# Moving the sample group's memory attention from the attention stage into the projection's second half

## The chip, the cores and the metric

The kernel runs on one core of one Trainium2 chip. The metric is the device time of one execution in microseconds (us): the median of several runs. One more execution is taken with the hardware profiler; all rows of "the profile" and "the trace" come from it.

## The reference

One layer of a hybrid decoder for a prompt of 2048 tokens and a sample group of 8 sequences of 4 new tokens each (8 x 4 = 32 rows). A combined projection `z = RMSNorm(x) @ w_in` gives eleven column groups of 512: `ca, cb, cg` (convolution), `pu, pg` (pooling), `q, k, v, sg` (stick-breaking attention), `mq, mg` (memory attention). Each branch is gated by its own SiLU path; the four branches are concatenated, multiplied by `w_out`, normalised and added to the residual.

The branch that the change touches is the memory attention of the sample group: each of the 8 sequences has its own 256 memory tokens, with keys `cache_mem_k` and values `cache_mem_v` of 4 heads x 128:

```python
def mem_attend(q, mk, mv):
    s = jnp.einsum('nqhd,nmhd->nhqm', q, mk).astype(jnp.float32) * (MEM_HEAD_DIM ** -0.5)
    p = jax.nn.softmax(s, axis=-1)
    return jnp.einsum('nhqm,nmhd->nqhd', p.astype(mv.dtype), mv)
...
y_m = mem_attend(mq.reshape(n, l, MEM_HEADS, MEM_HEAD_DIM), mk, mv).reshape(n, l, W_MEM)
mix = jnp.concatenate([..., y_m * jax.nn.silu(mg)], axis=-1)
```

## The kernel before

Three stages follow one another.

**Projection.** The normalised, transposed input lies in SBUF (`xhi`, `xlo`), 1024 prompt tokens plus the 32 sample rows in the first half (part 0), the other 1024 prompt tokens in the second (part 1). `z_groups` goes through column groups of 128: for each it runs `mm3` (24 matmuls on PE) per tile of up to 512 tokens into one of two PSUM banks (`z_tile`, pool `zps`), and `z_evac` empties the bank with ACT and DVE. It yields twice per tile; such a yield is called a step here. At each step `tasks.step()` lets every live task emit its next piece (turning rows, the prompt's memory attention `mem_attend`, pooling, the depthwise convolution `conv_dw` on DVE), and a planner (`due`, `rate`) lets the sample group's paged attention (`sample_stages`: gathers on POOL's queue, 32 x 32 turns on DVE, scores `sSA` and values `sO` on PE in strips) advance so that it ends shortly before the projection. Tasks take PSUM banks from a pool of three (`tp_tile`, pool `tps`), and SBUF tiles by tag: four of 4 KB per partition (`k4`), four of 2 KB (`small`).

The order of the instructions on PE is the order in which the code emits them. On the other engines the framework orders them by its own cost model and inserts all waits; each engine, and SP's DMA queue, then runs its list in order.

**Attention of the prompt.** `sb_prompt` walks over 4 head pairs x 4 query blocks of 512 tokens x key chunks. Per step: scores `S` on PE, gates `gam` and `be` on ACT, scans `E` on DVE, products on POOL, turns `AT` on PE, copies `at`, values `av` on PE, and at the end of a block one DVE instruction `sbo` (L1385). After the first eight steps `side_work` advances by one yield for every 4.0 cost units: first `sample_mem`, then `sample_end`, then the first output weights; then it waits until head pair 3 begins. Side work takes its PSUM banks from the two `AT` banks of `sb_prompt`. The `S` tiles (two banks each, two of them) lie in the PSUM space that `zps` and `tps` had.

**Output.** The products with `w_out`, the norm and the residual.

The sample group's memory attention is spread over these stages. In the first half the task `sample_keys` loads each sequence's keys (`mkb`, 512 KB) into a `k4` tile, turns them on PE (8 transposes, `smt`), copies them on ACT (`mkbT`) and stores them to DRAM (`mkTd`). It pauses while the prompt's memory attention is at work (`state["att"]`). `sample_mem`, in the attention stage, loads all turned keys, forms the scores of four sequences at a time in one bank (`smS`: per sequence four matmuls, one for each head, in 32-column strips; `qm` holds the queries with zeros at the other sequences' rows so that four sequences add up), adds the two banks into `smsc`, does the softmax, turns the probabilities (`smpt`), multiplies with the values of four sequences at a time (`smO`, all four heads against all 512 columns), masks the right head (`hm`), adds the heads (`smR`), turns the result (`smr`) and gates it into `mixs[3]`.

Of the kernel before, what the change touches and what calls it, by code (L numbers as in the profile page):

```python
# [18 lines left out]
P = 128  # L19
# [68 lines left out]
def kernel(  # L88
# [51 lines left out]
    mkTd = dram.tile([NB, P, 4, NMEM], F32, name="mkTd")  # L140
# [7 lines left out]
    zc = zx.enter_context(tc.tile_pool(name="zc", bufs=1, side="left"))  # L148
    zps = zx.enter_context(tc.tile_pool(name="zps", bufs=2, space=PSUM, side="left"))
    tps = zx.enter_context(tc.tile_pool(name="tps", bufs=3, space=PSUM, side="left"))  # L150
# [34 lines left out]
    us_s = zc.tile([P, 4, NB, CH + TS], F32, name="us_s")  # L185
    ps_s = zc.tile([P, 4, NB, PH + TS], F32, name="ps_s")
# [253 lines left out]
    def sample_keys():  # L440

        for b in range(NB):
            while state["att"]:
                yield
            k_ = k4(f"mkb{b}", [P, 2, 512], F32)
            sp.dma_start(k_, cmk[b].rearrange("(t p) c -> p t c", p=P))
            for _ in range(4):
                yield
            kT = k4(f"mkbT{b}", [P, 4, NMEM], F32)
            for t in range(2):  # L450
                pt = tp_tile(f"smt{b}_{t}")
                for h in range(4):
                    pe.transpose(pt[:, P * h : P * (h + 1)], k_[:, t, P * h : P * (h + 1)], ident)
                act.copy(kT[:, :, P * t : P * (t + 1)], pt.rearrange("p (h n) -> p h n", h=4))
                yield
            wq.dma_start(mkTd[b], kT)

# [159 lines left out]
    def conv_dw(c, U, part):  # L617
# [20 lines left out]
        if part == 0:  # L638
# [14 lines left out]
            wq.dma_start(ydw[c, :, SEQ : SEQ + NS], acc)  # L653

# [10 lines left out]
    state = {"att": 0}  # L665
# [168 lines left out]
    def state_rows(part):  # L834
        yield
        if part == 0:
            tcs = small("tcs")
            tps_ = small("tps")
            for t_, s_, o_ in ((tcs, us_s, CH), (tps_, ps_s, PH)):
                for c in range(4):  # L840
# [7 lines left out]
                      [(TS * b, TS * b + TS, pool_sample[0, b, PH - TS : PH, :]) for b in range(NB)])  # L848
        else:
# [297 lines left out]
    def sample_mem(sm, ps_, S):  # L1147

        qm = sm.tile([P, NB, 4, NS], F32, name="qm", bufs=1)
        pool.memset(qm, 0.0)  # L1150
        for b in range(NB):
            pool.tensor_copy(qm[:, b, :, TS * b : TS * (b + 1)], mqs[:, :, TS * b : TS * (b + 1)])

        h4 = sm.tile([P, 4, 4], F32, name="h4", bufs=1)
        pool.memset(h4, 1.0)
# [5 lines left out]
        for g in (2, 3):  # L1161
            pool.tensor_tensor(out=hm, in0=hm, in1=h4[:, g], op=ALU.add)
# [13 lines left out]
        for k in range(2):  # L1176
# [10 lines left out]
            for b in range(4 * k, 4 * k + 4):  # L1187
                vb[b] = load(b)
# [959 lines left out]
```

## Time and profile before

| | us |
|---|---|
| median of 3 runs | 2398.44 (2398.2 to 2399.28) |
| the profiled execution | 2395.7 |
| its span, first to last instruction | 2394.0 |
| first matmul of the second half's first tile (`z1k`) | 782.7 |
| last first-product matmul of the group `z1sg`, at the end of the projection | 1476.3 |
| last `sbo` of the attention | 1960.6 |

PE is TensorE's matmuls, PEld its weight loads, DVE VectorE, ACT ScalarE, POOL GpSimd, SP SyncE, which here only issues DMAs. `L1385` is line 1385 of the kernel. A form such as `128*32 128x256` of a matmul is its weights (rows * columns) and its moving operand. In the profile an fp32 matmul of two fp32 operands shows as two records; matmuls are pipelined, so a record lasts longer than the distance to the next one.

### The profile page before, as it was taken

What the parts mean: (1) busy time and instruction counts of PE and PEld (TensorE: products, weight loads), DVE (VectorE), ACT (ScalarE), POOL (GpSimd) and SP (SyncE); (2) the same over time, 40 slices, a digit from 0 to 9 for tenths busy, and PEclk for the clock granted to TensorE, in tenths of its full rate; (3) what the DMA queues carried; (4) which work ended last, traced back from release to release, by engine and by line L of the source; (5) the groups of instructions that cost most, each with busy time, mean ns of one, the idle gap of its engine ahead of it and who ended that gap; (6) DMA issues with size and microseconds to landing.
All of it is one profiled execution on the core that took longest, in us unless ns stands there. A gap on an engine that the chain in (4) does not pass through costs nothing. (4 is left out here: it accounts for less than half of the span.)

```text
span 2394.0 us, 42116 instructions
## 1 busy us (share of the span) xinstructions
PE 2275.1 (95%) x15962; PEld 1769.7 (74%) x15962; DVE 1732.6 (72%) x2420; ACT 1117.0 (47%) x1939; POOL 1286.6 (54%) x1323
## 2 busy tenths in 40 slices
PE   7899999999999999999999999899999998989996
PEld 7888888898888777777777776455555557778775
DVE  5332785959756764587877878879898846687998
ACT  5322343242442322224242435788989955443554
POOL 3454535556464655546556554667776754454430
PEclk9999999999999999999999999999999999999998
DMA  6678988887778899978878767834333217887764
GB/s 211 196 253 290 347 287 309 305 269 267 259 256 306 301 357 318 318 270 276 272 268 274 260 222 190 238 77 119 82 93 80 63 63 250 268 284 239 255 236 164
DMA packets 340437, 562.14 MB, mean 235 GB/s; under 512 B 28481, under 2 KB 212929, under 8 KB 323834
## 3 DMA queue, kind: packets, MB, share of 16 engines
q1 hardware_dynamic: 284858, 290.72, 39.2%
q0 software_dynamic: 55376, 268.72, 31.6%
q8 instruction: 126, 2.06, 0.3%
q14 instruction: 77, 0.63, 0.1%
HBM read 469.28 MB, written 90.68 MB: 234 GB/s over the span
## 5 line engine op out<-in xcount | busy, mean ns | idle before, releaser
L974 DVE STREAM_TRANSPOSE T<-kt 128x1024 f32<-128x1024 f32 x256 | 308.5, 1225 | 184.1 <-PE sSA L987 179.4
L941 POOL DMA_INDIRECT vt<-in_cache_v_dram,idv x256 | 252.8, 988 | 255.1 <-PE sO L1026 194.3
L629 DVE SCALAR_TENSOR_TENSOR cacc<-U,par,cacc 128x512 f32<-128x512 f32 x480 | 360.2, 750 | 11.5
L1353 POOL TENSOR_TENSOR be<-be,E 128x512 f32<-128x512 f32 (+3 forms) x316 | 301.2, 960 | 106.1 <-DVE E L1344 45.9
L1344 DVE TENSOR_TENSOR_SCAN E<-gam,cr,ZM 128x513 f32<-128x513 f32 x192 | 233.0, 1264 | 14.8 <-ACT gam L1275 13.5
L941 POOL DMA_INDIRECT kt<-in_cache_k_dram,idk x128 | 128.1, 1001 | 194.3 <-DVE T L974 155.0
L1364 PEld LDWEIGHTS AT<-ident,be 128*128 128x128 f32 x1082 | 115.7, 141 | 128.1 <-ACT at L1370 45.1
L1968 PE MATMUL acc<-wohi,mh 128*128 128x512 f32 (+1 forms) x480 | 194.6, 405 | 2.1 <-DVE mh L1725 1.1
L1275 ACT ACTIVATE gam<-S,nbias_bc 128x1024 f32<-128x1024 f32 (+1 forms) x158 | 171.6, 1086 | 46.0 <-ACT be L1276 17.1
L1968 PE MATMUL acc<-wolo,mh 128*128 128x512 f32 (+1 forms) x480 | 190.8, 397 | 0.0
L1968 PE MATMUL acc<-wohi,ml 128*128 128x512 f32 x448 | 179.0, 400 | 9.8 <-DVE ml L1725 9.6
L1271 PE MATMUL S<-kT,Q 128*128 128x512 f32 (+1 forms) x632 | 175.2, 401 | 4.6 <-DVE sg1sg L727 2.4
L1276 ACT ACTIVATE be<-S,bias_bc 128x1024 f32<-128x1024 f32 (+1 forms) x158 | 170.7, 1080 | 0.0
L1364 PE MATMUL AT<-ident,be 128*128 128x128 f32 x1082 | 156.3, 282 | 15.0 <-DVE at L1368 3.9
L1380 PE MATMUL av<-at,V 128*64 128x512 f32 (+3 forms) x640 | 152.6, 555 | 1.7 <-DVE sbo L1385 1.7
L987 PE MATMUL sSA<-T,W 128*32 128x128 f32 x4096 | 138.4, 276 | 3.2 <-DVE T L974 2.4
L987 PEld LDWEIGHTS sSA<-T,W 128*32 128x32 f32 x4096 | 104.1, 110 | 40.0 <-issue 31.1
L1725 DVE TENSOR_TENSOR ml<-mr,mh 128x512 fp32r<-128x512 f32 x108 | 98.6, 918 | 35.0 <-ACT mh L1714 34.6
L1026 PE MATMUL sO<-vt,saT 128*32 128x512 f32 x1024 | 122.3, 593 | 0.0
L1271 PEld LDWEIGHTS S<-kT,Q 128*128 128x128 f32 x632 | 105.6, 194 | 19.7 <-ACT be L1276 3.4
L1370 ACT COPY at<-AT 128x512 f32<-128x512 f32 x192 | 109.5, 661 | 14.4 <-PE AT L1364 14.4
L1341 DVE TENSOR_TENSOR_SCAN E<-gam,ZM 128x384 f32<-128x384 f32 (+1 forms) x124 | 94.5, 812 | 24.8 <-ACT gam L1275 22.1
(581 smaller groups left out, 6044.3 us busy)
## 6 DMA issues: line engine op xcount, KB each, us to landing
Q<-qd SPq DMA_DIRECT2D x64, 256.0 KB
mr<-mixd SPq DMA_DIRECT2D x32, 512.0 KB
mr<-mixd SPq DMA_DIRECT2D x48, 256.0 KB
wor<-in_w_out_dram SPq DMA_DIRECT2D x20, 512.0 KB
xtp<-in_x_prompt_dram SPq DMA_DIRECT2D x16, 512.0 KB
kT<-kd SPq DMA_DIRECT2D x64, 128.0 KB
wor<-in_w_out_dram SPq DMA_DIRECT2D x32, 256.0 KB
msd<-mr SPq DMA_DIRECT2D x32, 256.0 KB
```

The source lines that it names most:

```text
L629: dve.scalar_tensor_tensor(out=ps, in0=U[:, a + k : a + k + H], scalar=wd[:, k : k + 1], in1=ps, op0=ALU.mult, op1=ALU.add)
L941: pool.indirect_dma_start(out=dst, out_offset=None, in_=rows, in_offset=bass.IndirectOffsetOnAxis(ap=idx, axis=0))
L974: S["turn"] = dve.transpose(T[:, 2 * hh : 2 * hh + 2].rearrange("p s j t -> p (s j t)"), kt[:, 2 * hh : 2 * hh + 2].rearrange("p s j d -> ...
L987: pe.matmul(sSs[n][32 * g : 32 * g + 32, P * ml : P * (ml + 1)], lhsT=W[:, jj, :], rhs=T[:, :, jj, :], start=i == 0, stop=i == 3, tile_pos ...
L1271: pe.matmul(S[:, j, :w], lhsT=Q[:, x, P * (q2 + j) : P * (q2 + j + 1)], rhs=kt[:, :w], start=x == 0, stop=x == 1)
L1275: act.activation(out=ga, in_=S[:, :, :w], func=AF.Sigmoid, bias=nbias_bc[:, h : h + 1], scale=-1.0)
L1276: act.activation(out=be, in_=S[:, :, :w], func=AF.Sigmoid, bias=bias_bc[:, h : h + 1])
L1344: dve.tensor_tensor_scan(out=E[:, j][:, ::-1], data0=g_[:, j][:, ::-1], data1=ZM[:, 0:1].to_broadcast([P, 513]), initial=carry[hh, q2][:, ...
L1353: pool.tensor_tensor(out=be[:, j, :m], in0=be[:, j, :m], in1=E[:, j, 513 - w : 513 - w + m], op=ALU.mult)
L1364: pe.transpose(ap_[:, P * qt : P * (qt + 1)], A[hp, qb, kc, hh, qt][:, P * r : P * (r + 1)], ident)
L1380: pe.matmul(av[64 * hh : 64 * hh + 64, c], lhsT=V[:, 4 * kc + r, 64 * hh : 64 * hh + 64], rhs=ats.pop((hp, qb, kc, r, hh))[:, c], start=dg ...
L1968: pe.matmul(o[:rows], lhsT=m[a][:, k, :rows], rhs=W[prod, 4 * h + k][w], start=not cont and h == k == n == 0, stop=h == 1 and k == 3 and n ...
```

## The change

`sample_keys` and the scratch `mkTd` go. `sample_mem` becomes a task of the projection, added after the key and value groups of the second half, and does everything there. Per sequence: the rows (keys, later values) are loaded one sequence ahead of their use; the keys are turned and copied as before, the scores of this one sequence go into a `tp_tile` bank, and DVE adds them up. After the softmax each sequence's values are multiplied in four strips of 256 columns: two token halves times two pairs of heads, at four partition groups of one bank. ACT copies the bank, and two matmuls against a selector (`Sel`, 128 x 8 ones and zeros) turn it, add the two token halves and pick the right head in one go; DVE gates the result.

For its long-lived tiles it takes the space of the sample's convolution and pooling histories (`us_s`, `ps_s`), so it waits until these are read (`state["early"]` counts four convolutions and two state rows). And the PSUM pool of the turned tiles (`tps`) is opened before that of the projection's output (`zps`), so the two change places among the banks.

```diff
-    mkTd = dram.tile([NB, P, 4, NMEM], F32, name="mkTd")
...
+    tps = zx.enter_context(tc.tile_pool(name="tps", bufs=3, space=PSUM, side="left"))
     zps = zx.enter_context(tc.tile_pool(name="zps", bufs=2, space=PSUM, side="left"))
-    tps = zx.enter_context(tc.tile_pool(name="tps", bufs=3, space=PSUM, side="left"))
...
-    def sample_keys():
...
-    def sample_mem(sm, ps_, S):
...
+    def sample_mem():
+
+        while state["early"] < 6:
+            yield
+        qm = zc.tile([P, NB, 4, NS], F32, tag="us", name="qm", bufs=1)
+        pool.memset(qm, 0.0)
         for b in range(NB):
             pool.tensor_copy(qm[:, b, :, TS * b : TS * (b + 1)], mqs[:, :, TS * b : TS * (b + 1)])
...
+        def rows(src, b, nm):
+            while state["att"]:
+                yield
+            t = k4(f"{nm}{b}", [P, 2, 512], F32)
+            sp.dma_start(t, src[b].rearrange("(t p) c -> p t c", p=P))
             return t

+        ahead = yield from rows(cmk, 0, "mkb")
+        for _ in range(4):
+            yield
         for b in range(NB):
+            k_ = ahead
+            ahead = yield from (rows(cmk, b + 1, "mkb") if b + 1 < NB else rows(cmv, 0, "mvb"))
+            kT = k4(f"mkbT{b}", [P, 4, NMEM], F32)
+            for t in range(2):
+                pt = tp_tile(f"smt{b}_{t}")
                 for h in range(4):
+                    pe.transpose(pt[:, P * h : P * (h + 1)], k_[:, t, P * h : P * (h + 1)], ident)
+                act.copy(kT[:, :, P * t : P * (t + 1)], pt.rearrange("p (h n) -> p h n", h=4))
+                yield
+            yield
+            S = tp_tile(f"smS{b}")
+            for h in range(4):
+                pe.matmul(S[32 * h : 32 * h + 32, :NMEM], lhsT=qm[:, b, h, :], rhs=kT[:, h, :], start=True, stop=True,
+                          tile_position=(0, 32 * h))
+            if b:
                 dve.tensor_tensor(out=sc, in0=sc, in1=S[:, :NMEM], op=ALU.add)
             else:
                 dve.tensor_copy(sc, S[:, :NMEM])
...
+        for b in range(NB):
+            k, g = divmod(b, 4)
+            v_ = ahead
+            if b + 1 < NB:
+                ahead = yield from rows(cmv, b + 1, "mvb")
+            O = tp_tile(f"smO{b}")
             for t in range(2):
+                for c in range(2):
+                    r = 64 * t + 32 * c
+                    pe.matmul(O[r : r + 32, :256], lhsT=pv[:, t, g], rhs=v_[:, t, 256 * c : 256 * c + 256], start=True,
+                              stop=True, tile_position=(0, r))
+            Os = small(f"smOs{b}")
+            act.copy(Os[:, :256], O[:, :256])
+            yield
+            yield
+            yield
+            pt = tp_tile(f"smr{b}")
+            for n in range(2):
+                pe.matmul(pt[:, 2 * TS * n : 2 * TS * (n + 1)], lhsT=Os[:, P * n : P * (n + 1)],
+                          rhs=Sel[:, k, n].rearrange("p c q -> p (c q)"), start=True, stop=True)
+            heads = lambda x: x[:, :, TS * b : TS * (b + 1)].rearrange("p (c n) q -> p n c q", c=2)
+            dve.tensor_tensor(out=heads(mo), in0=pt[:, : 4 * TS].rearrange("p (n c q) -> p n c q", n=2, c=2),
+                              in1=heads(gms), op=ALU.mult)
         sp.dma_start(mixs[3], mo)
...
-        yield from z_groups(0, GROUPS[0][12:14])
-        tasks.add(sample_keys())
-        yield from z_groups(0, GROUPS[0][14:])
+        yield from z_groups(0, GROUPS[0][12:])
         tasks.add(state_rows(0))
-        yield from z_groups(1, GROUPS[1][:-2])
+        yield from z_groups(1, GROUPS[1][:7])
+        tasks.add(sample_mem())
+        yield from z_groups(1, GROUPS[1][7:-2])
...
-        for i, part in enumerate((sample_mem, sample_end)):
-            with tc.tile_pool(name=f"sm{i}", bufs=1, side="left", reuse_waits="tile") as sm2:
-                yield from part(sm2, side_ps, S)
+        with tc.tile_pool(name="sm", bufs=1, side="left", reuse_waits="tile") as sm2:
+            yield from sample_end(sm2, side_ps, S)
```

108 lines of the change are left out of this document (26 added, 82 removed).

## Prediction

> **What bounds the kernel now.** I read the page first, then the busy times by stretch of the span, then PE's timeline at the two places that the change touches: the projection's second half, where it puts the work, and the first 150 us of the attention, where it takes the work away. The page:
>
> ```profile
> span 2394.0 us, 42116 instructions
> PE 2275.1 (95%) x15962; PEld 1769.7 (74%) x15962; DVE 1732.6 (72%) x2420; ACT 1117.0 (47%) x1939; POOL 1286.6 (54%) x1323
> ```
>
> PE is busy 95% of the span, but that is a mean over stages. By stretch (columns: length, then busy us of PE, PEld, DVE, ACT and POOL with their instruction counts, then granted clock, DMA share, GB/s):
>
> ```profile
> 320.00:380.00 60.00, 55.21 (x491) 48.80 (x492) 47.57 (x73) 35.26 (x66) 28.15 (x29) 1.00 0.75 262
> 1000.00:1200.00 200.00, 199.81 (x1512) 148.36 (x1505) 159.14 (x207) 56.16 (x99) 108.09 (x98) 1.00 0.80 272
> ```
>
> The second row is the projection's second half: PE has no idle time (199.81 of 200), while DVE, ACT, POOL and the DMA engines all have some. Whatever PE work is added here moves the end one for one. The first row is where the key transposes of the sample's memory run now, beside a memory head of the prompt: there PE loses 4.79 of 60 us.
>
> The next view is the timeline of PE at the start of the attention, where the scores of the sample's memory (smS) run now. Columns: start, length, engine, line, operation, and in brackets PE's idle time before and what ended it.
>
> ```profile
> 1494.94 0.66 PE L1364 MATMUL AT<-ident,be 128*128 128x128 f32 x4
> 1497.21 0.64 PE L1181 MATMUL smS<-mkbT,qm 128*32 128x256 f32 x8 [1.61 <-DVE at L1368]
> ...
> 1501.74 2.08 PE L1271 MATMUL S<-kT,Q 128*128 128x512 f32 x4
> ...
> 1506.27 1.93 PE L1181 MATMUL smS<-mkbT,qm 128*32 128x256 f32 x32
> 1508.13 0.65 PE L1380 MATMUL av<-at,V 128*64 128x256 f32 x4
> 1508.72 0.66 PE L1364 MATMUL AT<-ident,be 128*128 128x128 f32 x4
> 1511.00 0.63 PE L1364 MATMUL AT<-ident,be 128*128 128x128 f32 x4 [1.62 <-DVE smsc L1184]
> ```
>
> PE's own work ends at 1495.60, then it waits for a bank, works and waits on smS until 1501.74 (6.14 us), gives 1.86 us more from 1506.27, and waits 1.62 us for DVE to empty the bank: 9.62 us of PE for the scores. But PE is not alone there. DVE in the same stretch:
>
> ```profile
> 1484.12 1.00 DVE L1341 TENSOR_TENSOR_SCAN E<-early,ZM 128x128 f32<-128x128 f32 x2 [4.21 <-ACT ZM L1301]
> ...
> 1501.87 0.42 DVE L1186 COPY smsc<-smS 128x256 f32<-128x256 f32 x1 [0.91 <-PE smS L1181]
> 1505.34 0.49 DVE L1368 TENSOR_TENSOR at<-AT,tri 128x128 f32<-128x128 f32 x2 [3.04 <-PE AT L1364]
> 1510.46 0.40 DVE L1184 TENSOR_TENSOR smsc<-smsc,smS 128x256 f32<-128x256 f32 x1
> 1510.89 0.42 DVE L1190 TENSOR_REDUCE smx<-smsc 128x1 f32<-128x256 f32 x1
> ```
>
> From 1484.12 DVE works through its scans almost without a gap; its idle time that smS causes is 0.91 + 3.04 us, and the instructions that go away here are 0.42 + 0.40 + 0.42. So the start-up could be held by DVE rather than PE.
>
> **The change, part by part.**
>
> *Attention, scores.* Out go 9.62 us of PE, but DVE would then be late next: it can move up only by 0.91 + 3.04 + 0.42 + 0.40 + 0.42 = 5.2 us. Bounds 5.2 and 9.6; I take 5.2, because DVE has no other gap there. The sample's last attention part (sample_end) moves up into this place. It has the same instructions as now and takes the same kind of bank; I cost the move at nothing, at worst the 1.61 us bank wait of the smS row.
>
> *Attention, values.* For these I use a yardstick: the instruction that finishes a block of 512 queries of a head pair (sbo, DVE). First head pair, then the third, which has no side work:
>
> ```profile
> 1535.38 0.67 DVE L1385 TENSOR_TENSOR sbo<-av,sgt 128x512 f32<-128x512 f32 x1
> 1574.79 0.66 DVE L1385 TENSOR_TENSOR sbo<-av,sgt 128x512 f32<-128x512 f32 x1
> ...
> 1768.07 0.67 DVE L1385 TENSOR_TENSOR sbo<-av,sgt 128x512 f32<-128x512 f32 x1
> 1800.81 0.67 DVE L1385 TENSOR_TENSOR sbo<-av,sgt 128x512 f32<-128x512 f32 x1
> ```
>
> The same block takes 39.41 us beside the values of the sample's memory and 32.74 us without: 6.7 us go. What is late next is PE itself, as in the clean block.
>
> *PSUM banks.* The attention's first score tile takes the first two banks on the left. Before, these are the two of the projection's output; after, two of the turned tiles, which are free earlier.
>
> ```profile
> 1479.96 3.13 PE L1271 MATMUL S<-kT,Q 128*128 128x512 f32 x8 [2.39 <-DVE sg1sg L727]
> 1481.48 1.12 ACT L1275 ACTIVATE gam<-S,nbias_bc 128x1024 f32<-128x1024 f32 x1 [1.14 <-PE S L1271]
> ```
>
> PE's wait of 2.39 us for the gate sg1sg goes. What is late next is ACT, which waited only 1.14 us for these scores; and DVE's first scan waits for ZM, which ACT makes after these gates. So 1.1 us, at most 2.4, at least 0.
>
> Together the attention gives 5.2 + 6.7 + 1.1 = 13.0 us, at most 9.6 + 6.7 + 2.4 = 18.7. That the later side parts (sample_end, the first output weights) end sooner is worth nothing: in the code they then wait for head pair 3.
>
> *Projection, the strips.* Added to PE's full stream are eight score groups and eight value groups, each 8 matmul records of 256 columns in four strips side by side. What such a group costs inside the stream shows where the paged attention (sSA, 32 records of 128 columns in four strips) interrupts it now; below it, a 128-row, 128-column weight load with a short moving operand, like the new matmuls by the selector:
>
> ```profile
> 1417.64 0.39 PE L243 MATMUL z1mq<-xlo,whi1mq 128*128 128x512 f32 x1
> 1417.87 0.40 PE L243 MATMUL z1mq<-xhi,wlo1mq 128*128 128x512 f32 x1
> 1418.20 1.08 PE L987 MATMUL sSA<-T,W 128*32 128x128 f32 x32
> 1419.21 0.50 PE L243 MATMUL z1mq<-xhi,whi1mq 128*128 128x512 f32 x1
> 1419.55 0.40 PE L243 MATMUL z1mq<-xlo,whi1mq 128*128 128x512 f32 x1
> ...
> L904 PE MATMUL qps<-qsT,rep x32: 192/276/277, 140.0 to 143.4; 128*128 128x32 f32 x32
> ```
>
> The stream's step is 0.23 us (1417.64 to 1417.87). From 1417.87 to 1419.55 are 1.68 us, of which two steps are the stream's own 0.46: the interruption costs 1.22. Its columns alone are half of the long smS run (1.86 us for as many records of twice the columns): 0.93. So 0.29 us are the price of going to strips and back. A group of 8 records is a quarter of the long run, 0.47 us, plus 0.29 when it stands alone: 0.76. Sixteen make 7.5 us (no price of switching) to 12.2 us; I take 12.2, because before, each switch was paid for 16 or 32 records and now for 8.
>
> The Trainium skill, "TensorEngine Tiling (Array Packing)", Key Properties, says that changing the tiling mode drains TensorE; it gives no figure, and by it the sum is that of the upper end, with which the sSA row agrees.
>
> *Projection, the selector.* Each batch adds two matmuls of 8 columns against a 128-column weight, 4 records in fp32; 32 in all. The qps row has 32 records in 3.4 us between first and last start: 0.11 us each, so 3.5 us. Below, nothing excludes that their weight loads hide behind the stream: 0.
>
> The same page, Instruction Overhead, puts about 60 cycles on each short matmul, which at the 2.4 GHz of "TensorE: Matmul & The Clock Gate" is an estimate of 0.8 us for 32 and would make the sum below 2.7 us lower; the qps row has far more.
>
> *What moves without a new price.* The 64 key transposes go from the first half to the second: the same instructions in a stream that is full in both. The seven DVE adds, the eight ACT copies of the value strips, POOL's clearing of qm and its selects go beside 159, 56 and 108 busy us of 200 in the 1000 to 1200 row. If that cover were gone, their length would count. A small wait moves with the transposes:
>
> ```profile
> PE py L608 <- ACT mkbT L454: 1.2, 1, 1.2
> SPq L729 <- DVE sg1sg L727: 33.0, 3, 16.0
> ```
>
> PE waited 1.2 us in the first half behind the copies of the turned keys; I take 1.2 out there and 1.2 in for the second half. Bounds: up to 4.8 out (all that PE loses from 320 to 380) and up to 4.8 in.
>
> *DMA.* Eight loads of keys and eight of values, 512 KB each, 8.4 MB, go into the second half; the turned keys' trip to DRAM and back (8.4 MB) goes altogether. At 272 GB/s and a share of 0.80, the 200 us row leaves 68 GB/s, 13.6 MB: covered. SP issues in order, and a row load can stand behind a wait of up to 16.0 us (the second line above) that SP has there for a gate; the load has three steps before its use.
>
> ```profile
> L652 ACT ACTIVATE accs<-accs,par x4: 321/322/341, 368.2 to 938.3; 128x32 f32<-128x32 f32 x4
> L243 PE MATMUL z1k<-xhi,whi1k x64: 388/393/502, 782.7 to 852.6; 128*128 128x512 f32 x64
> L243 PE MATMUL z1sg<-xhi,whi1sg x64: 389/393/792, 1070.0 to 1476.3; 128*128 128x512 f32 x64
> ```
>
> The second half has 44 x 2 tiles of two steps, 176 steps in 694 us: 3.94 us a step, 11.8 us for three. The task may start after 938.3 (the last sample convolution) and needs some 61 steps, 240 us, plus its pauses for the memory heads: it ends long before 1476.
>
> *The sum.* Projection 12.2 + 3.5 + 1.2 - 1.2 = +15.7; attention -13.0; together +2.7 us. The profiled execution took 2395.7 us (its span and 1.7 us around it), so 2398.4 for its like; the median of the runs, 2398.44, lies 2.7 us above it and becomes 2401.1. A measurement of this kernel can tell about 0.2% (4.8 us) from no change, so this is no change.
>
> **The rivals.**
>
> *The attention gives all of PE's time.* If DVE can catch up, the scores give 9.6 us; if the groups fall next to the paged attention's own strips, they cost 7.5. Then 7.5 + 3.5 - 18.7 - 1.2 = -8.9, 2389.5 us. For it: PE, not DVE, is the full engine later in the attention, and sSA and sO groups come every few steps. Against: DVE's gap of 3.95 us is all that it has.
>
> *Buffers in the second half become the wait.* The task holds two to three of the four k4 slots, and one of the four small slots for three steps of each value batch. The prompt's memory heads and gates want the same slots, so an ACT or DVE instruction that empties a projection tile waits for a slot, those queued behind it wait in order, and with two output banks PE stops. The price is that of the row 320 to 380, where keys and a memory head met before: 4.8 us; the values meet two such heads, 2 x 4.8 + 2.7 = +12.3, 2410.7 us. It decides from 2.1 us of PE idle time between 940 and 1250 on, beyond what the sum has. For it: that row, and the 16.0 us wait on SP. Against: from 1000 to 1200 PE loses 0.19 us, so there is much slack.
>
> *The task isn't hidden.* If it started late or paused too long, the rest would run after the projection's last tile, when nothing else is on PE: some batches of three steps, 11.8 us each, one batch giving 2401.1 + 11.8 = 2412.9. The 240 us against 538 speak against it.
>
> **How the numbers follow.** The balance near zero 0.42: within 0.2% in 0.32, slower in 0.08, faster in 0.02; its own range is 2396 to 2407. All of PE's time 0.27, all faster. Buffers 0.28 and not hidden 0.03, all slower. So faster 0.29, same 0.32, slower 0.39. The range reaches to the first two rivals with a little of their spread: 2388 to 2411.
>
> **What would show it.** In the changed kernel's trace: PE's last projection matmul about 16 us later than 1476 (terms of the strips and the selector: the gap in the stream around each group 0.76 us, around each selector pair 0.44); PE's waits from 940 to 1250 under 3 us; the first S without its wait for sg1sg; the first sbo and the block of 39.41 us shorter by about 6 and 7 us; the attention about 13 us shorter. Wrong would be: waits of PE on ACT or DVE for banks in the second half that add to more than 5 us; an attention that gives over 18 us, or under 8; a change in the output stage, where I expect none.

## The result and the profile after

The changed kernel takes 2395.1 us (median of 22 runs, 2390.37 to 2400.3), the kernel before 2398.97 in the same comparison (22 runs, 2395.63 to 2406.97): a ratio of 0.9978, interval 0.9969 to 0.9987. That is faster by 0.22%, at the edge of what such a measurement tells from no change. The prediction said 2401.1 and no change. The time lies in its range, but it moved the other way: forecast +2.7 us, measured -3.9. A second comparison (below) put the two kernels within 0.1% of each other, so the size of the change can't be read from one pair of medians. Two single executions on record, of 4414.94 and 9874.47 us, stand far outside all others and are in no median here.

The page of the changed kernel. Its profiled execution took 2398.75 us, 3.65 above its median, and the profiled execution before 3.27 below the median beside it, so the two spans can't be set against each other as a whole:

```profile
span 2397.0 us, 42257 instructions
PE 2282.8 (95%) x16024; PEld 1773.7 (74%) x16024; DVE 1726.2 (72%) x2428; ACT 1118.6 (47%) x1947; POOL 1287.5 (54%) x1322
```

The two stretches that the prediction showed, from the busy times by stretch (length; busy us of PE, PEld, DVE, ACT, POOL; granted clock, DMA share, GB/s):

```profile
320.00:380.00 60.00, 57.93 (x502) 51.03 (x501) 49.04 (x75) 28.25 (x54) 30.46 (x31) 1.00 0.72 229
1000.00:1200.00 200.00, 199.90 (x1579) 146.84 (x1569) 150.68 (x207) 61.66 (x112) 102.64 (x92) 1.00 0.82 283
```

With the key transposes gone, PE loses 2.07 us of 60 in the first stretch where it lost 4.79. In the second the whole task now runs, and PE still loses nothing (199.90 of 200), with the DMA share at 0.82 where it was 0.80. So buffers and transfers did not become the wait.

Where the time is, by the first and last starts of two groups (before, then after):

```profile
L243 PE MATMUL z1q<-xhi,whi1q x64: 388/393/500, 914.4 to 971.8; 128*128 128x512 f32 x64
```

```profile
L242 PE MATMUL z1q<-xhi,whi1q x64: 388/392/499, 909.0 to 968.8; 128*128 128x512 f32 x64
L242 PE MATMUL z1sg<-xhi,whi1sg x64: 388/392/796, 1077.9 to 1490.9; 128*128 128x512 f32 x64
```

Up to z1q the changed kernel is 5.4 us ahead; from z1q to the end of z1sg it takes 581.9 us where the kernel before takes 561.9 (1476.3 - 914.4). The projection ends 14.6 us later; the forecast was 15.7.

The attention gives that back. PE's timeline at its start:

```profile
1492.02 1.98 PE L1253 MATMUL S<-kT,Q 128*128 128x512 f32 x8
1496.99 0.73 PE L1253 MATMUL S<-kT,Q 128*128 128x256 f32 x4 [2.99 <-ACT be L1258]
1499.52 2.93 PE L1253 MATMUL S<-kT,Q 128*128 128x512 f32 x8 [1.79 <-ACT be L1258]
...
1510.69 0.69 PE L1062 MATMUL nS<-ksT,qz 128*32 128x32 f32 x16 [1.40 <-DVE at L1350]
```

The first S starts without its wait for sg1sg, as forecast. What is late next is ACT: PE waits 2.99 and 1.79 us for gates. The moved-up sample_end (nS) waits 1.40 us for its bank, near the 1.61 that smS waited there. DVE's first scan:

```profile
1497.46 1.00 DVE L1323 TENSOR_TENSOR_SCAN E<-early,ZM 128x128 f32<-128x128 f32 x2 [2.88 <-ACT ZM L1283]
```

It still waits for ZM from ACT, 2.88 us where it was 4.21. The ends of the blocks (sbo), after:

```profile
1521.47 0.65 DVE L1367 TENSOR_TENSOR sbo<-av,sgt 128x512 f32<-128x512 f32 x1
1544.35 0.67 DVE L1367 TENSOR_TENSOR sbo<-av,sgt 128x512 f32<-128x512 f32 x1
1581.70 0.66 DVE L1367 TENSOR_TENSOR sbo<-av,sgt 128x512 f32<-128x512 f32 x1
...
1734.54 0.69 DVE L1367 TENSOR_TENSOR sbo<-av,sgt 128x512 f32<-128x512 f32 x1 [0.19 <-PE av L1362]
...
1960.34 0.69 DVE L1367 TENSOR_TENSOR sbo<-av,sgt 128x512 f32<-128x512 f32 x1 [7.64 <-PE av L1362]
```

and before:

```profile
1512.96 0.69 DVE L1385 TENSOR_TENSOR sbo<-av,sgt 128x512 f32<-128x512 f32 x1 [0.28 <-PE av L1380]
...
1734.72 0.69 DVE L1385 TENSOR_TENSOR sbo<-av,sgt 128x512 f32<-128x512 f32 x1 [0.19 <-PE av L1380]
1960.59 0.69 DVE L1385 TENSOR_TENSOR sbo<-av,sgt 128x512 f32<-128x512 f32 x1 [7.64 <-PE av L1380]
```

From the last z1sg to the first sbo are 30.6 us, before 36.7: 6.1 given. From the first to the eighth sbo are 213.1 us, before 221.8: 8.7 given. Together 14.8, and at the end of the attention the kernels stand 0.25 us apart. The block of 39.41 us, which the forecast expected 7 shorter, takes 37.35: sample_end runs in it now.

### The profile page after: what moved, and what is told of

It is laid out like the page before. It is cut to its first block, busy times and chain, and to the rows that moved or that the text cites. A ratio compares the mean times of both kernels' runs of the same rounds, so it can differ in the third digit from the quotient of the medians.

```text
span 2397.0 us, 42257 instructions
## 1 busy us (share of the span) xinstructions
PE 2282.8 (95%) x16024; PEld 1773.7 (74%) x16024; DVE 1726.2 (72%) x2428; ACT 1118.6 (47%) x1947; POOL 1287.5 (54%) x1322
## 3 DMA queue, kind: packets, MB, share of 16 engines
q8 instruction: 126, 2.06, 0.3%
## 5 line engine op out<-in xcount | busy, mean ns | idle before, releaser
L1352 ACT COPY at<-AT 128x512 f32<-128x512 f32 x192 | 110.2, 670 | 12.2 <-PE AT L1346 12.2
```

## The experiments

All kernels were read by the same stages, in us, worked out from first and last starts as above (the last column is the median of the runs). By the record the two repeats and the two kernels without the branch ran on chip 8, the edits of banks and scratch on chip 14 and the last four kernels on chip 0; for the first comparison no chip is named:

| kernel | to z1q | z1q to end of z1sg | to last sbo | output | span | median |
|---|---|---|---|---|---|---|
| before | 914.4 | 561.9 | 484.3 | 433.4 | 2394.0 | 2398.97 |
| before again | 915.3 | 561.7 | 483.8 | 431.9 | 2392.7 | 2396.21 |
| before, new bank order | 907.7 | 561.7 | 484.9 | 435.7 | 2390.0 | 2397.67 |
| before, scratch last | 914.7 | 561.7 | 487.4 | 434.9 | 2398.7 | 2395.56 |
| before, no values | 909.9 | 561.9 | 477.3 | 437.6 | 2386.7 | 2392.26 |
| after | 909.0 | 581.9 | 469.4 | 436.7 | 2397.0 | 2395.1 |
| after again | 908.2 | 581.1 | 469.4 | 434.8 | 2393.5 | 2396.05 |
| after, old bank order | 903.8 | 581.2 | 470.4 | 439.9 | 2395.3 | 2395.45 |
| after, scratch kept | 905.0 | 581.3 | 469.3 | 437.5 | 2393.1 | 2394.74 |
| no branch, old banks | 903.8 | 561.9 | 471.1 | 435.5 | 2372.3 | 2374.52 |
| no branch, new banks | 905.7 | 562.1 | 471.1 | 436.8 | 2375.7 | 2374.23 |
| keys only, new place | 903.5 | 571.4 | 470.2 | 429.4 | 2374.5 | 2379.56 |
| after, no selector | 904.5 | 579.7 | 470.5 | 440.1 | 2394.8 | 2390.83 |
| after, strips beside and ZM on DVE | 909.8 | 579.7 | 467.8 | 437.8 | 2395.1 | 2391.26 |

The second column repeats within 0.2 us for the kernels with the branch at its old place (561.7 to 561.9) and within 0.8 for the changed kernel and its variants with other banks and scratch (581.1 to 581.9). The third repeats within 1.1 us after the change, but spreads by 3.6 us before it (483.8 to 487.4). So single profiles can tell terms of a microsecond from z1q to z1sg and in the attention after the change, and not in the attention before it. The runs spread by 3 us (standard deviation).

**Both kernels again, unchanged.**

> The kernel before, unchanged, for a second profiled execution. The profiles taken so far differ by 14.6 us at the projection's end (1476.3 and 1490.9), by 0.25 us at the last but one block of the attention (1910.54 and 1910.29) and by 3.0 us at the end the other way, while the medians of 22 runs differ by 3.9 us in favour of the change. Theory A (the balance of the prediction: projection and attention times are fixed, the spread of the runs comes from the output stage): projection end and block times again within 0.3 us, the time from the block at 1910 to the end not 483.5 but several us away from it, about 487. Theory B (the projection varies from execution to execution): projection end more than 2 us away from 1476.3.

> The changed kernel, unchanged, for a second profiled execution. Theory A: projection end 1490.9 and block 1910.3 again within 0.3 us, the output stage shorter than the 486.7 us of the first profile, about 483. Theory B: projection end more than 2 us away from 1490.9.

Measured beside 23 shared runs of the kernel before (2398.18): before again 2396.21, ratio 0.9991 (0.9979 to 1.0002); after again 2396.05, ratio 1.0001 (0.9991 to 1.001). The two medians stand 2.0 and 2.1 us below the shared runs, although the first is of the kernel before itself: it differs from itself by as much as the change moved it there. Over all comparisons in which the kernel before or the changed kernel ran unedited, 117 runs before have a median of 2398.18 and 34 after 2395.65: 2.5 us, 0.11%.

Neither theory came out as written. The projection ends 0.7 us later and 1.6 us earlier than in the first profiles, where A wanted 0.3 and B more than 2, and from the block at 1910 to the end are 481.9 and 484.9 us, where A expected about 487 and 483. From z1q to the last sbo either kernel repeats within 0.8 us. Where the executions differ is the output, but also the time up to z1q (907.7 to 915.3 for kernels that keep the old placement), which A had not said.

**Without the branch, in both bank orders.** The gates go into the output in the branch's place.

```diff
-        tasks.add(sample_mem())
...
     def sample_end(sm, ps_, S):
+        sp.dma_start(mixs[3], gms)
```

> The sample group's memory attention is left out altogether (the gates stand in for its result), PSUM pools in the order of before. It prices the attention's old place: time of before minus this. Balance theory: 64 transposes (7 us) and 1 us of waits in the first half, 13 us in the attention, so about 21 us less than before, 2378; projection end about 1468, first S still with its wait of 2.4 us. Rival (the attention loses all of PE's 16.3 us for scores and values plus clock): 2374 or less.

> As the last one (memory attention left out), but with the PSUM pools in the order of the change. It prices the new place: time of after minus this, and the banks: the last one minus this. Balance theory: after minus this is 7 (transposes) + 13 to 16 (strips and selector) = 20 to 23 us, about 2374; the banks give 1.1 us. Rival (the banks give more, since the clock no longer drops at the start of the attention): 3 us or more between the two.

Ratios to the kernel before: 0.9908 (0.9892 to 0.9923) and 0.9902 (0.9888 to 0.9917). The medians on this chip, 2374.52 and 2374.23, lie 23.7 us below the shared runs of the kernel before and 21.8 below the changed kernel: the branch costs some 22 us at either place, the change moves a cost, and it is worth the small difference of two large terms. The first of them misses the balance theory's 2378 and stands 0.5 us above the bound of its rival, 2374. By stages 9.2 us are saved up to z1q (mean 913.0 of four kernels with the old placement, less 903.8), where 8 were expected, and 14.0 in the attention (485.1 less 471.1) where 13 were. The banks, for which 1.1 us was expected between the two kernels, give nothing: the attention takes 471.1 us with either order. After the change the attention (469.4 us) is even shorter than without any branch, so nothing of the branch's cost is left in it.

**The bank order alone.**

```diff
+    zps = zx.enter_context(tc.tile_pool(name="zps", bufs=2, space=PSUM, side="left"))
     tps = zx.enter_context(tc.tile_pool(name="tps", bufs=3, space=PSUM, side="left"))
-    zps = zx.enter_context(tc.tile_pool(name="zps", bufs=2, space=PSUM, side="left"))
```

> The changed kernel with the two PSUM pools in their old order. In the profiles so far the first DVE scan starts 6.6 us after the projection's last first-product matmul with the new order (changed kernel twice, and without the branch) and 7.8 to 8.3 us with the old one. Forecast's theory (the banks' term is worth 1.1 us at the attention's end): first S waits 2.4 us for sg1sg, first scan at 7.8 to 8.3 us, second sbo at 54.9 us after the projection's end instead of 53.4, median 1 to 1.5 us above the changed kernel's. Rival (the 1.5 us are given back before the second block ends, as the pair without the branch suggests: 55.1 and 54.9 us): first scan later by 1.5 us, second sbo within 0.5 us of 53.4, median within 1 us of the changed kernel's 2396.

> The kernel before with the two PSUM pools in the changed kernel's order, nothing else. Forecast's theory: first S without its wait for sg1sg, first scan 6.6 us after the projection's last first-product matmul instead of 7.8 to 8.0, second sbo 57.0 us after it instead of 58.1 or more (59.1 and 57.4 before), median 1.1 us below the kernel before. Rival (given back in the first two blocks): second sbo unchanged, median within 1 us of the kernel before.

In the changed kernel with the old order the first S waits again:

```profile
1488.74 2.11 PE L1253 MATMUL S<-kT,Q 128*128 128x512 f32 x8 [2.37 <-DVE sg1sg L709]
```

Its first scan starts 7.7 us after the projection's end (1492.67 - 1485.0) instead of 6.6, its second sbo 54.4 instead of 53.4 us, its last 470.4 instead of 469.4: the order is worth 1.0 us here, the forecast's 1.1. In the kernel before, the new order also brings the first scan forward (6.6 us), but the second sbo comes 59.1 us after the projection's end, as in the first profile, and the attention takes 484.9. No gain shows there; as that sbo came at 57.3 to 60.2 us in the three profiles with the old order, a gain of 1.1 us could also be lost in the spread. The medians (ratios 0.999, 0.9978 to 1.0003, and 1.0004, 0.9994 to 1.0015) can't show a microsecond.

**The place of the scratch in DRAM.** The forecast expected no change in the output stage; the first profiles showed 3 us more.

```diff
 (kernel before)
-    mkTd = dram.tile([NB, P, 4, NMEM], F32, name="mkTd")
...
     msd = dram.tile([2, 8, 2, P, 4, P], F32, name="msd")
+    mkTd = dram.tile([NB, P, 4, NMEM], F32, name="mkTd")
 (changed kernel)
+    mkTd = dram.tile([NB, P, 4, NMEM], F32, name="mkTd")
...
+        sp.dma_start(mkTd[0, :, :, :NS], mo)
```

> The kernel before with one edit that issues no instruction: the 4 MB scratch for the turned keys is declared behind the other scratch tensors, so these lie 4 MB lower in DRAM, as they do in the changed kernel. From the last sbo to the end of the span the two profiles of the kernel before show 433.4 and 431.9 us, the changed kernel 436.7 and 434.8, the two kernels without the branch 435.5 and 436.8, although every engine has the same instructions in the same order there. Theory P (the place of the scratch in DRAM sets it): this kernel shows 435 to 437 us there, median 2 to 4 us above the kernel before. Theory C (it differs from execution to execution): 431 to 434 or anything, median within 1.5 us of the kernel before.

> The changed kernel with the scratch for the turned keys declared at its old place, so that the other scratch tensors lie in DRAM where the kernel before has them; so that it stays in use, one 64 KB store of the finished branch goes into it, behind the store that is there. Theory P (place in DRAM): from the last sbo to the end 431.5 to 433.5 us instead of 434.8 and 436.7, median 2 to 4 us below the changed kernel, so 2392 to 2394. Theory C: within 1.5 us of the changed kernel, 2395 to 2397. The extra store is worth nothing in both: the queue has over a fifth of its time free there.

434.9 and 437.5 us in the output. Theory P falls: with the scratch back at its old place the stage did not become shorter. Ratios 0.9995 (0.9982 to 1.0008) and 0.9994 (0.9982 to 1.0006). Over all fourteen profiles the stage takes 429.4 to 440.1 us, the shortest and the longest in two edits of the changed kernel on one chip. In the first two profiles, 433.4 and 436.7 us, PE, DVE, ACT and POOL have the same instructions in the same order there. The stage differs from execution to execution, and what decides it stays open; so does whether some of the 3 us between the means of the first four kernels of either sort (434.0 and 437.2) belongs to the change.

**The keys' part alone, and all but the selector.** The first leaves out scores, softmax, values and selector, the second the selector and the products behind it.

```diff
 (keys only: sample_mem ends behind the turns)
-            S = tp_tile(f"smS{b}")
-            ...
+        sp.dma_start(mixs[3], gms)
 (no selector)
-            pt = tp_tile(f"smr{b}")
-            for n in range(2):
-                pe.matmul(pt[:, 2 * TS * n : 2 * TS * (n + 1)], lhsT=Os[:, P * n : P * (n + 1)],
-                          ...
-            dve.tensor_tensor(out=heads(mo), ...)
+        sp.dma_start(mixs[3], gms)
```

> The changed kernel with only the keys' part of the branch at its new place: the 8 loads, 64 transposes and their copies stay; scores, softmax, values and selector are left out, and the gates go into the output in the branch's place. Stage read: from the first matmul of z1q to the last first-product matmul of z1sg, 561.9 and 562.1 us without the branch, 581.1 to 581.9 us in four profiles of the changed kernel and its variants. Theory M (prices read from the stream of the changed kernel: 0.44 us for each set of 4 transposes, so 16 x 0.44 = 7.0 us): 568.9 to 569.5 us. The forecast's step (the transposes move without a new price, because they cost as much in the first half) says nothing of the price itself, but if they hid in the first half's idle time, before this stage the kernel before would lose less than 7 us against the kernel without the branch. Rival (the loads' DMA or waits for slots cost in the second half): above 571.

> The changed kernel without its 16 selector matmuls (32 records) and the 8 DVE products behind them: the strips' results are copied and not used, and the gates go into the output in the branch's place. Same stage, 581.1 to 581.9 us with them. Forecast's term (32 x 0.11 = 3.5 us; 0.44 us for each pair in the stream): 577.6 to 578.4 us. Rival (their weight loads hide behind the stream): above 580. Together with the kernel that keeps the keys' part alone this gives the strips: theory M (5.2 us for the scores' groups and 4.0 for the values' groups, beside the two turns of the probabilities of 0.2 us each) expects 8.8 to 9.8 us between the two kernels, the forecast's 16 x 0.76 12.2 us.

Keys only, with the two groups and PE's first wait from 900 to 1470 us (us in total, times, longest):

```profile
L242 PE MATMUL z1q<-xhi,whi1q x64: 388/392/499, 903.5 to 962.7; 128*128 128x512 f32 x64
L242 PE MATMUL z1sg<-xhi,whi1sg x64: 388/392/792, 1068.6 to 1474.9; 128*128 128x512 f32 x64
```

```profile
PE smt L1151 <- DMA mkb<-in_cache_mem_k_dram: 2.5, 1, 2.5
```

571.4 us, in the rival's range, and the wait tells why: one load of keys landed 2.5 us late. No profile of the full task shows that wait. Without it the stage takes 568.9, which is theory M's 7.0 us for the turns. The lead of three steps is enough, but not by much. The ratio is 0.9925 (0.9901 to 0.9949, four runs).

Without the selector:

```profile
L242 PE MATMUL z1q<-xhi,whi1q x64: 388/392/499, 904.5 to 964.3; 128*128 128x512 f32 x64
L242 PE MATMUL z1sg<-xhi,whi1sg x64: 388/392/792, 1073.6 to 1484.2; 128*128 128x512 f32 x64
```

579.7 us: by the stage's length the selector is worth 1.4 to 2.2 us (581.1 to 581.9 less 579.7), between the forecast's 3.5 and nothing. But here PE has two waits of 0.3 us each on DVE (for `mh1mq` and `smrest`) that no profile with the selector has. By PE's busy time in the stage, 577.15 us beside 579.29 to 580.00 in four profiles with the selector, it is 2.1 to 2.9 us. The two kernels stand 10.8 us apart without the late load (579.7 - 568.9); less 0.4 for the two turns of the probabilities, the sixteen strip groups cost 10.4 us: not 12.2, and not the 9.2 behind theory M either. The ratio is 0.9966 (0.9952 to 0.9979).

**The strips beside the paged attention's, and ZM on DVE.**

```diff
 (end of a score group of the paged attention)
+            while pend:
+                pend.pop(0).pop()()
 (sample_mem: each score and value group becomes a function f)
+        def beside(f):
+            job = [f]
+            pend.append(job)
+            for _ in range(8):
+                if not job:
+                    return
+                yield
+            if job:
+                pend.remove(job)
+                f()
...
-        act.copy(ZM, zm)
+        dve.tensor_copy(ZM, zm)
```

> The changed kernel with two edits. (1) The score and value groups of the branch are emitted right behind a score group of the paged attention, which is in strips as well, instead of alone in the stream. In the changed kernel a group alone costs 0.72 us (score groups) or 0.67 (value groups), one beside the paged attention 0.59 or 0.44, one between its scores and its values 0.3. Theory M: stage from z1q's first to z1sg's last first-product matmul 1 to 2 us shorter than 581.1 to 581.9. If the price of going to strips and back were all that a group costs beside its columns (forecast: 0.29 of 0.76), 16 x 0.29 = 4.6 us less at most. Rival: no change, or longer, because the task holds its slots for longer. (2) ZM is copied by DVE instead of ACT: in the changed kernel DVE waits 2.88 us for ACT's copy ahead of its first scan. Theory: the first scan starts 4.2 to 4.6 us after the projection's last first-product matmul instead of 6.6, and the second sbo at 51 to 52.5 us after it instead of 53.4. Rival: ACT's gates, for which PE waits 2.99 and 1.79 us, hold the start, and the second sbo gains 0.5 us, the length of the copy on ACT, or nothing. Sum: 2 to 4 us below the changed kernel, 2391.5 to 2394 us.

DVE at the start of the attention:

```profile
1493.23 0.70 DVE L1305 COPY ZM<-zm 128x512 f32<-128x512 f32 x1
1493.96 1.00 DVE L1345 TENSOR_TENSOR_SCAN E<-early,ZM 128x128 f32<-128x128 f32 x2
```

Both edits did what was expected: the stage from z1q takes 579.7 us (1.4 to 2.2 less), the first scan starts 4.5 us after the projection's end (1493.96 - 1489.5) and the second sbo comes 51.5 us after it instead of 53.4. All sixteen groups stand beside the paged attention's in this stream. Of the stage's gain 0.8 to 1.5 us are PE's busy time (578.52 beside 579.29 to 580.00); the rest is idle time of PE, 1.2 us where it was 1.8 to 1.9. The median is 2391.26 us beside 2399.15 for 26 runs of the kernel before: ratio 0.9964 (0.995 to 0.9978). That beats the kernel before. The changed kernel was not run in this comparison; its 34 runs in the others have a median of 2395.65. Some 3 to 4 us of the distance are seen in the two stages, the rest is the change and the spread.

**The kernel before without the values' part.** The loads, 16 matmuls, masks, sums and turns of the values are left out.

```diff
-            for b in range(4 * k, 4 * k + 4):
-                vb[b] = load(b)
...
-        for k in range(2):
-            O = ps_(f"smO{k}")
-            ...
+        sp.dma_start(mixs[3], gms)
```

> The kernel before without the values' part of the sample's memory attention: the loads of values, 16 matmuls, masks, sums and turns are left out, and the gates go into the output in the branch's place; turned keys, scores, softmax and the turn of the probabilities stay. Stage read: from the projection's last first-product matmul to the last sbo of the attention, 484.3, 483.8, 484.9 and 487.4 us in four profiles of the kernel before and its variants, 469.3 to 470.4 in four of the changed kernel and its variants. Forecast's split (6.7 us for the values, from the one block of 39.41 us): 477.6 to 478.5 us. Theory M (5.8 us for all ahead of the first sbo, and 9.6 for what comes behind it, spread over the blocks from the second to the seventh because the side parts behind it move up too): 474.5 to 476 us. In both the first sbo stays at 34.9 to 37.7 us after the projection's end.

```profile
1506.75 0.69 DVE L1360 TENSOR_TENSOR sbo<-av,sgt 128x512 f32<-128x512 f32 x1 [0.28 <-PE av L1355]
...
1949.06 0.69 DVE L1360 TENSOR_TENSOR sbo<-av,sgt 128x512 f32<-128x512 f32 x1 [7.64 <-PE av L1355]
```

From the projection's end (1471.8) to the last sbo are 477.3 us, and to the first 35.0. Neither split holds as written: the 477.3 us lie above theory M's 474.5 to 476 and 0.3 below the forecast's 477.6 to 478.5, which is less than the spread of the kernels it is set against. Against the mean of the four kernels with the branch in its old place (485.1, 483.8 to 487.4) the values are worth 7.8 us (6.5 to 10.1). Of these, 6.3 (5.3 to 7.4) lie behind the first sbo, where the values' products run (from 1541.94 on in the kernel before); the rest lies ahead of it, where the four kernels differ among themselves by 2.8 us.

What remains to the changed kernel's 469.6 (mean of four) is 7.7 for scores, softmax and banks. Theory M had put all that comes behind the first sbo down to the values. Some of it belongs to the scores: of the 7.7, 3.5 lie in the block from the third to the fourth sbo, which takes 47.62 us here (1566.38 to 1614.00) and 44.13 in the changed kernel (1581.70 to 1625.83). Here it has the last products of sample_end in it (`nyn` at 1577.49), which the changed kernel has one block earlier (1542.04). That the scores' steps push sample_end back would explain it, but wasn't tried by itself. The ratio is 0.9975 (0.9963 to 0.9987).

## Why the prediction was right and wrong

The mechanism was right: a full PE pays for all that is added to the projection, the attention gives about as much, and the rest is a small difference. The step that failed is the sum of the terms, and with it the sign: +2.7 us became -2.4 up to the end of the attention. Three of its terms stood near the end of their bounds that speaks against the change, and a fourth did not come. The strips were put at the top of 7.5 to 12.2 us, with a switch for each of the sixteen groups; they measured 10.4. Scores and banks were put at 6.3, near the bottom of 5.2 to 12.0, because DVE was thought to hold the start and the move of sample_end was costed at nothing; they measured 7.7. The selector's 3.5 was 1.4 to 2.9, and the wait of 1.2 at the turned keys did not come. Only the time up to z1q went the other way, by 1.7. The sizes:

| term (us) | forecast | measured (means of four kernels of each sort) |
|---|---|---|
| up to z1q: turns and their wait leave | -8.2 (7.0 and 1.2) | -6.5 (913.0 to 906.5) |
| from z1q: turns arrive | +7.0 | +7.0 |
| strips | +12.2 | +10.4 |
| selector | +3.5 | +1.4 to 2.2 (2.1 to 2.9 by PE's busy time) |
| wait at the turned keys | +1.2 | none |
| attention | -13.0 | -15.5 (485.1 to 469.6) |
| sum | +2.7 | -2.4 |

The forecast left the 7.0 out on both sides, as equal, and had no term for the two turns of the probabilities, 0.4 us. The measured sum is made from the stage means (up to z1q -6.5, from z1q +19.6, attention -15.5); the medians over all runs differ by 2.5 us. "Four kernels" are two profiles of the kernel itself and one of each of its variants with other banks and another scratch.

That -2.4 and -2.5 agree is luck in part. The term up to z1q comes from profiles that spread by 7.6 us with the keys in the first half (907.7 to 915.3, five profiles) and 6.3 without (903.5 to 909.8, nine). And the sum leaves out the output stage: its means of 434.0 and 437.2 would add 3.2 and make it +0.8, as the spans of the four profiles do (means 2393.9 and 2394.7). So the stages show the sizes of the terms between z1q and the last sbo, -15.5 against +19.6, but not the sign of the whole; for that there are only the medians, 3.9 and 2.1 us apart in two comparisons, the second with a ratio of 1.0001 all the same.

The first rival, by which the attention gives all of PE's time and the groups fall next to the paged attention's, came half true: 2395.1 us lies between its 2389.5 and the balance's 2401.1, the attention gave 15.5 us between 13.0 and 18.7, and the strips cost 10.4 between 12.2 and 7.5. The other two rivals did not come: PE waited 0.4 us from 940 to 1250, for no bank, and the task's last matmuls start at 1219.56 us, long before 1490.9.

*Strips.* The price of one was right, the rule that every group pays it was not. In the changed kernel's stream, a score group ahead of a set of turns, the turns alone, and a score group beside the paged attention:

```profile
962.09 0.40 PE L242 MATMUL z1q<-xhi,wlo1q 128*128 128x512 f32 x1
962.42 0.64 PE L1172 MATMUL smS<-mkbT,qm 128*32 128x256 f32 x8
962.99 0.66 PE L1166 MATMUL smt<-ident,mkb 128*128 128x128 f32 x4
963.40 0.48 PE L242 MATMUL z1q<-xhi,whi1q 128*128 128x512 f32 x1
963.71 0.39 PE L242 MATMUL z1q<-xlo,whi1q 128*128 128x512 f32 x1
...
966.03 0.39 PE L242 MATMUL z1q<-xhi,wlo1q 128*128 128x512 f32 x1
966.26 0.60 PE L1166 MATMUL smt<-ident,mkb 128*128 128x128 f32 x4
966.62 0.47 PE L242 MATMUL z1q<-xhi,whi1q 128*128 128x512 f32 x1
966.93 0.39 PE L242 MATMUL z1q<-xlo,whi1q 128*128 128x512 f32 x1
...
1049.14 0.40 PE L242 MATMUL z1pg<-xhi,wlo1pg 128*128 128x512 f32 x1
1049.46 0.64 PE L1172 MATMUL smS<-mkbT,qm 128*32 128x256 f32 x8
1049.92 1.06 PE L970 MATMUL sSA<-T,W 128*32 128x128 f32 x32
1051.07 0.49 PE L242 MATMUL z1pg<-xhi,whi1pg 128*128 128x512 f32 x1
1051.40 0.40 PE L242 MATMUL z1pg<-xlo,whi1pg 128*128 128x512 f32 x1
```

From the last matmul of the stream ahead of an interruption to the second behind it, less two steps of 0.23: 1.16 us in the first case and 0.44 in the second, so 0.72 for the strips (forecast 0.76). In the third 1.80, of which 1.22 are the paged attention's: 0.58. The value groups, in the kernel without the selector, beside the paged attention and alone:

```profile
1129.27 0.40 PE L242 MATMUL z1cb<-xhi,wlo1cb 128*128 128x512 f32 x1
1129.59 0.64 PE L1198 MATMUL smO<-mvb,smrest 128*32 128x256 f32 x8
1130.05 1.06 PE L970 MATMUL sSA<-T,W 128*32 128x128 f32 x32
1131.04 0.50 PE L242 MATMUL z1cb<-xhi,whi1cb 128*128 128x512 f32 x1
1131.37 0.39 PE L242 MATMUL z1cb<-xlo,whi1cb 128*128 128x512 f32 x1
...
1164.69 0.40 PE L242 MATMUL z1cg<-xhi,wlo1cg 128*128 128x512 f32 x1
1165.01 0.64 PE L1198 MATMUL smO<-mvb,smrest 128*32 128x256 f32 x8
1165.58 0.50 PE L242 MATMUL z1pg<-xhi,whi1pg 128*128 128x512 f32 x1
1165.92 0.39 PE L242 MATMUL z1pg<-xlo,whi1pg 128*128 128x512 f32 x1
```

By the same working 1.64 - 1.22 = 0.42 us beside, 0.77 alone. Where a step of the task and one of the paged attention put their strips directly behind each other, the way to strips and back is paid once. In the changed kernel's stream that is so for one of the eight score groups (1049.46; the others stand ahead of turns) and four of the eight value groups (1070.22, 1133.72, 1144.27 and 1206.03). Seven times 0.72, once 0.58, four times 0.77 and four times 0.42 make 10.4 us, which is what the stage showed. The prediction had named this case ("if the groups fall next to the paged attention's own strips") and given it to a rival instead of taking part of it into the sum. The Trainium skill, "TensorEngine Tiling (Array Packing)", Key Properties, says that a change of the tiling mode drains TensorE; these rows agree: a group that shares its switch saves 0.14 us (scores) or 0.35 us (values).

*Selector.* 0.11 us for each record came from a row of 32 such records one behind the other. In the changed kernel's stream a pair stands ahead of a value group:

```profile
1169.48 0.40 PE L242 MATMUL z1cg<-xhi,wlo1cg 128*128 128x512 f32 x1
1169.71 0.51 PE L1215 MATMUL smr<-msel,smOs 128*128 128x8 f32 x4
1170.15 0.64 PE L1206 MATMUL smO<-mvb,smrest 128*32 128x256 f32 x8
1170.72 0.50 PE L242 MATMUL z1pg<-xhi,whi1pg 128*128 128x512 f32 x1
1171.05 0.40 PE L242 MATMUL z1pg<-xlo,whi1pg 128*128 128x512 f32 x1
```

1.11 us, of which 0.77 are the value group's: 0.34 for the pair where the forecast had 0.44, 2.7 for eight. PE's busy time in the stage says 2.1 to 2.9, which agrees; the stage's length says 1.4 to 2.2, because the kernel without the selector waits 0.6 us more.

*The wait for turned keys* did not come in the second half. All that PE waits between 940 and 1250 in the changed kernel (us in total, times, longest):

```profile
PE sSA L970 <- ACT saT L999: 0.4, 1, 0.4
```

The rival of the buffers needed 2.1.

*Attention, scores.* The bound by DVE (5.2 us) fits the start, but the start is not all. The first sbo moved by 6.1 us with the banks in it, as forecast (6.3). The kernel without values shows 7.7 for scores, softmax and banks: 4.4 ahead of the first sbo (35.0 less 30.6), which is within DVE's bound, and 3.3 behind it, where the forecast had put the move of sample_end at nothing. That lies inside the bounds (5.2 to 12.0 for scores and banks together), and the value was taken too near to their lower end.

*Attention, values.* The term was 6.7 us, measured 6.3 behind the first sbo and 7.8 over the whole attention. The yardstick, one block beside the values against the same block without side work, was sound for its size but not for its place: sample_end moved into that block, which gave only 2.06 us, and the blocks behind gave the rest. "The move at nothing" fails for that block. Whoever had looked at the block of 39.41 us alone would have called the term refuted.

*Banks.* 1.1 forecast; 1.0 measured in the changed kernel. In the pair without the branch the two orders end alike (471.1 us), and in the kernel before no gain shows. So the term is confirmed in one pair of three, and why the pair without the branch gives it back stays open.

*Output stage.* "None expected" can neither be confirmed nor refuted within the 429.4 to 440.1 us that it takes; the 3.2 us between the means are larger than the whole sum of the other stages.

## What to carry to other kernels

When work moves from one full stage to another, the result is a difference of terms that are ten times as large: price each term by the interruption it makes in the stream, with its neighbours in it, and give the sum an error of its terms' size before naming a sign. In this stream a group of strips cost 0.72 to 0.77 us alone and 0.42 to 0.58 directly ahead of another, so emit groups of one form back to back; with all sixteen so placed the stage was 1.4 to 2.2 us shorter, for a few lines of code. Look last at the engine that the first dependent instruction waits for: moving one 0.6 us copy from ACT, which was busy, to DVE, which waited for it, brought the first scan forward by 2.1 us, of which 1.6 were left at the end of the attention.

## What the runs showed of the hardware

Two things were not expected. The output stage, whose code no edit touched, took 429.4 to 440.1 us in fourteen profiles, and the time up to z1q spread by 7.6 us among five kernels with the keys at their old place, while the 562 us between z1q and the projection's end repeated within 0.2 us. And a 512 KB load of keys was late once, by 2.5 us, in the lighter kernel that turned the keys and did nothing else: it was issued at 954.05 us, and PE came to it at 967.6, 13.5 us later.
